# The delta rule's keys turned token-major by VectorE block transposes and a DRAM round trip instead of by TensorE

## The chip, the cores and the metric

One core of a Trainium2 chip runs the whole kernel. The metric is the device time of one execution in microseconds (us); a kernel is judged by the median of several executions. In rows of the profile PE is TensorE's matmul, PEld its weight load, DVE is VectorE, ACT is ScalarE, POOL is GpSimd, and SP is SyncE, which issues nearly all DMAs here.

## The reference, cut to what matters

One layer of a hybrid decoder block, 1024 tokens, model width 1024, everything in float32. The input projection `h @ W_in` gives the columns of two mixers; the first one is a gated delta rule with 8 heads of width 128.

```python
qkv = causal_dwconv_silu(concatenate([qa, ka, va]), conv_w)      # 4 taps along the tokens
k_dn = l2_normalize(ka.reshape(b, s, 8, 128))                    # x * rsqrt(sum(x*x) + EPS)
g    = -exp(a_log) * softplus(a_in + dt_bias);  beta = sigmoid(beta_in)
# chunks of tokens, gc = cumsum(g) in a chunk, decay[i, j] = exp(gc[i] - gc[j]) for j <= i
lmat  = where(strict, (k * beta) @ k.T * decay, 0)
t_inv = inverse(eye + lmat)
u, w  = t_inv @ (v * beta), t_inv @ (k * beta * exp(gc))
a_qk  = q @ k.T * decay
k_dec = k * exp(gc[-1] - gc)
for each chunk:                                                  # state: 128 x 128 per head
    v_new = u - w @ state
    o     = (q * exp(gc)) @ state + a_qk @ v_new
    state = state * exp(gc[-1]) + k_dec.T @ v_new
```

Then `rms_norm(o) * silu(z)` goes through a projection, a dilated window attention (the second mixer) through another, both are gated, added, sent through `w_out`, added to the input and normalized.

## The kernel before, in words

**The work on TensorE.** Every big product is split in two float32r halves and done as three matmuls of 128x128 by 128x512 (`three`, line 557; the tiles `pj`). `projections` (line 724) runs one unit of 48 such matmuls after another in the order of the list `prog`: for each pair of heads p the keys k0 and k1, then q, v, z tiles and some gates; then the attention's tiles; then the products behind both mixers. Weights come by DMA into `wr` (2 tiles) and are split by ScalarE and VectorE into `wh` (6 tiles). A unit's result leaves PSUM by ScalarE and, for q, k and v, by three VectorE multiply-adds (`conv`, line 577).

**The delta rule** of a head is a set of generators ("streams"). The keys leave `conv` channel-major: 128 channels on partitions, 1024 tokens along the free axis. `k_stream` (line 896) needs them token-major, as `kp` (128 tokens of a chunk on partitions, 8 chunks of 128 channels along the free axis), for two things: the sum of squares of each token (`kss`, which gives `s_all` and `ds_all`, the normalized beta and its decayed form) and the weights of the state update. It does this by 8 TensorE transposes into two PSUM tiles `sb`; ScalarE takes 8 squares with a running sum, and copies the two halves to `kp`; GpSimd multiplies `kp` by `ds_all`. `d_stream` makes the decay tile, `n_stream` multiplies keys by keys (and on VectorE by `s_all`), `inv_stream` inverts 32x32 blocks of two heads at once on VectorE (31 steps), `merge_stream` puts them together to the inverse `TT`, `q_stream` and `qsum_stream` do the same for the queries, and `v_stream` turns the values token-major by `turn` (line 1082): a VectorE block transpose, a DMA to DRAM and four DMAs back, which end in another order of the free axis (4 blocks of 32 channels outermost). `rec_stream` (line 1107) then walks over 8 chunks: two products with the state (`kt`, `qt` by `st`), a VectorE step to `r`, a product with `TT`, a ScalarE copy to `w`, two products with `kp` and the attention tile `at`, and a VectorE step to the next state. The two heads of a pair run in each other's gaps.

**What sets the order.** The kernel runs no scheduler on the chip. While it is written, `Sched` (line 103) keeps a clock for each engine, books each instruction with a cost (`book`, line 123), and lets the ready stream of the lowest priority number go on; `projections` has number 99 and fills what is left. Each engine then has its instructions in that order and waits at each only for its own inputs. What a stream does there is bound by tile slots: `Slots.get` (line 60) waits until a tile is free, and with `add=n` until more than `debt + n` are free. The pool `big` has 34 tiles of 128x1024; a key projection asks with `add` 4 or 3 (`out_store`, line 696), since the streams of its pair will take that many, and a head gives five tiles back when its last chunk is written:

```python
        while len(self.free_at) <= (0 if add is None else self.debt + add):   # 62, Slots.get
        add = dict(kA=4 - idx % 2, qA=1, qB=(4, 0, 4, 0, 4, 0)[idx % 6]).get(kind, 0)   # 699
        big.put(5)                                                            # 1163, rec_stream
```

Of the kernel before, what the change touches and what calls it, by code (L numbers as in the profile page):

```python
# [7 lines left out]
F32 = mybir.dt.float32  # L8
F32R = mybir.dt.float32r
AF = mybir.ActivationFunctionType  # L10
OP = mybir.AluOpType
AX = mybir.AxisListType
# [3 lines left out]
P = 128  # L16
T = 1024
D = 1024
H = 8
# [233 lines left out]
def hybrid_block_kernel(ctx: ExitStack, tc: tile.TileContext, x, c, norm_w, ada_w, ada_b, w_tiles, w_vb0, w_vb1,  # L253
# [3 lines left out]
    pe, act, dve, pool, sp = S.pe, S.act, S.dve, S.pool, S.sp  # L257
# [9 lines left out]
    dp = ctx.enter_context(tc.tile_pool(name="dram", bufs=1, space=DRAM))  # L267
    ctx.enter_context(tc.manual_schedule())

    big = Slots(S, bigp, "big", NBIG, [P, T])  # L270
# [5 lines left out]
    sb = Slots(S, sbp, "sb", 4, [P, 512])  # L276

    def const(shape, name, dtype=F32):
        return cp.tile(shape, dtype, name=name)
# [3 lines left out]
    ident, upper, later, ones = cst[:, 0:128], cst[:, 128:256], cst[:, 256:384], cst[:, 384:512]  # L283
# [18 lines left out]
    ds_all = const([P, 64], "ds_all")  # L302
# [11 lines left out]
    fg_d = [dp.tile([32, P], F32, name=f"fgd{g}") for g in range(3)]  # L314
    g_d = dp.tile([64, P], F32, name="grow")
    ot_d = [dp.tile([P, T], F32, name=f"otd{h}") for h in range(H)]
    vt_d = [dp.tile([P, T], F32, name=f"vtd{h}") for h in range(H)]
    st_d = dp.tile([T, 3, 8], F32, name="std")

# [546 lines left out]
    kss = const([P, H, 8], "kss")  # L866
# [4 lines left out]
    junk2 = const([P, P], "junk2")  # L871
# [24 lines left out]
    def k_stream(h):  # L896
        yield ev_k[h]
        yield ev_stats
        kt = KT[h]
        hs = slice(h * 8, h * 8 + 8)  # L900
        kp = yield from big.get(owed=1)
        for hf in range(2):
            pb = yield from sb.get()
            for i in range(4):
                pe.transpose(pb[:, i * P:(i + 1) * P], kt[:, (4 * hf + i) * P:(4 * hf + i + 1) * P], ident)
            yield
            for i in range(4):
                act.activation(junk2, pb[:, i * P:(i + 1) * P], AF.Square, accum_out=kss[:, h, 4 * hf + i:4 * hf + i + 1])
            act.activation(kp[:, hf * 512:hf * 512 + 512], pb, AF.Copy)
            sb.put()  # L910
        yield
        t = ik[:, h]
        dve.tensor_scalar(t, kss[:, h], EPS, None, op0=OP.add)
        dve.reciprocal(s_all[:, hs], t)
        dve.tensor_tensor(s_all[:, hs], s_all[:, hs], beta[:, hs], op=OP.mult)
        dve.tensor_tensor(ds_all[:, hs], s_all[:, hs], dec[:, hs], op=OP.mult)
        S.set(ev_s[h])
        yield
        pool.tensor_tensor(t, t, pw[:, 1], op=OP.pow)
        kp3 = kp.rearrange("p (a b) -> p a b", a=8)  # L920
        pool.tensor_tensor(kp3, kp3, ds_all[:, hs, None].to_broadcast([P, 8, P]), op=OP.mult)
        KP[h] = kp
        S.set(ev_kp[h])

# [157 lines left out]
    def turn(src, dst, bounce):  # L1082

        t = yield from big.get()
        dve.transpose(t.rearrange("p (j i d) -> p i j d", j=4, i=8), src.rearrange("p (i j d) -> p i j d", i=8, j=4))
        yield
        sp.dma_start(bounce, t)
        big.put()  # L1090
        yield
        bv = bounce.rearrange("(b r) (j f) -> j r b f", b=4, j=4)
        for j in range(4):
            sp.dma_start(dst[32 * j:32 * j + 32, :].rearrange("r (b f) -> r b f", b=4), bv[j])
        yield
# [540 lines left out]
    for h in range(H):  # L1636
        S.add(rec_stream(h), 3 + h * 0.01, f"rec{h}")
        S.add(merge_stream(h), 3.5 + h * 0.01, f"merge{h}")
        S.add(v_stream(h), 4 + h * 0.01, f"v{h}")
        S.add(q_stream(h), 4.2 + h * 0.01, f"q{h}")  # L1640
        S.add(qsum_stream(h), 4.3 + h * 0.01, f"s{h}")
        S.add(n_stream(h), 4.4 + h * 0.01, f"n{h}")
        S.add(k_stream(h), 4.6 + h * 0.01, f"k{h}")
        S.add(d_stream(h), 4.8 + h * 0.01, f"d{h}")
# [78 lines left out]
```

## Time and profile before

| What | Value |
|---|---|
| median of three executions | 1302.91 us (1300.87 to 1303.49) |
| the profiled execution | 1300.81 us, of which its span is 1299.0 us |
| TensorE matmul busy | 1261.6 us (97% of the span) |
| VectorE, ScalarE, GpSimd busy | 690.9, 494.3 and 145.4 us |
| DMA | 137.65 MB, 106 GB/s in the mean |
| granted TensorE clock, mean | 0.994 |

All engine instructions are recorded through one helper, so that every row names line 96; rows are told apart by their tiles. `pj<-big,wh` is a matmul of a projection, `sb<-cst,big` a transpose (of h at the start, of the keys later), `sb<-big` keys by keys, `sb<-sq,big` and `sb<-sq,TT` the recurrence of a head, `sb<-qpart,cst` the sum of the queries' squares, `vtd` and `otd` the DRAM tiles through which values and outputs are turned, `grow` a row of decays that is spread over partitions. A float32 matmul of 128x128 stands as two records. The time of the profiled execution is 2.1 us under the median.

### The profile page before, as it was taken

What the parts mean: (1) busy time and instruction counts of PE and PEld (TensorE: products, weight loads), DVE (VectorE), ACT (ScalarE), POOL (GpSimd) and SP (SyncE); (2) the same over time, 40 slices, a digit from 0 to 9 for tenths busy, and PEclk for the clock granted to TensorE, in tenths of its full rate; (3) what the DMA queues carried; (4) which work ended last, traced back from release to release, by engine and by line L of the source; (5) the groups of instructions that cost most, each with busy time, mean ns of one, the idle gap of its engine ahead of it and who ended that gap; (6) DMA issues with size and microseconds to landing.
All of it is one profiled execution on the core that took longest, in us unless ns stands there. A gap on an engine that the chain in (4) does not pass through costs nothing.

```text
span 1299.0 us, 18858 instructions
## 1 busy us (share of the span) xinstructions
PE 1261.6 (97%) x7386; PEld 1049.0 (81%) x7386; DVE 690.9 (53%) x1437; ACT 494.3 (38%) x1054; POOL 145.4 (11%) x97
## 2 busy tenths in 40 slices
PE   5799899999999999999999999999999999999997
PEld 3698678988888988888888888777777888888886
DVE  6766682377763468843778533232322147645433
ACT  5637312455234362234542242453536342222211
POOL 4601200023000221001310002000000000002400
PEclk9899999999999999999999999999999999999999
DMA  9335532163321433231522226211100257333422
GB/s 362 120 123 179 95 93 58 33 197 94 95 70 40 149 125 93 78 102 33 179 74 73 82 66 194 66 35 65 35 33 33 83 187 208 102 127 117 156 95 89
DMA packets 76138, 137.65 MB, mean 106 GB/s; under 512 B 30193, under 2 KB 43921, under 8 KB 76050
## 3 DMA queue, kind: packets, MB, share of 16 engines
q1 hardware_dynamic: 75906, 136.20, 33.2%
q8 instruction: 58, 0.95, 0.3%
q14 instruction: 30, 0.25, 0.1%
q10 hardware_dynamic: 144, 0.26, 0.1%
HBM read 105.84 MB, written 30.59 MB: 105 GB/s over the span
## 4 chain that ended last, share of the span: by engine, by line
PE 82%; issue 7%; DVE 6%; DMA 3%; POOL 1%; ACT 1%; SPq 0%; POOLq 0%; DVEq 0%; ACTq 0%
PE pj L96 69%; PE sb L96 13%; DVE big L96 4%; DMA big<-in_x_dram 1%; DMA vtd<-big 1%; DVE wh L96 1%; POOL big L96 1%; DVE mod L96 1%; DMA big<-grow 0%; ACT big L96 0%; DVE mid L96 0%; DMA big<-otd 0%; SPq L96 0%; POOL mo L96 0%; DMA otd<-big 0%
## 5 line engine op out<-in xcount | busy, mean ns | idle before, releaser
L96 PE MATMUL pj<-big,wh 128*128 128x512 f32 x3840 | 941.8, 398 | 11.2 <-POOL big L96 6.4
L96 PEld LDWEIGHTS pj<-big,wh 128*128 128x128 f32 x3840 | 706.3, 189 | 157.5 <-POOL big L96 7.8
L96 ACT ACTIVATE wh<-wr 128x1024 fp32r<-128x1024 f32 (+3 forms) x96 | 95.6, 996 | 316.1 <-PE pj L96 292.4
L96 DVE TENSOR_TENSOR wh<-wr,wh 128x1024 fp32r<-128x1024 f32 (+3 forms) x93 | 115.5, 1243 | 148.1 <-ACT wh L96 147.9
L96 ACT ACTIVATE big<-big 128x1024 f32<-128x1024 f32 (+1 forms) x61 | 64.5, 1059 | 147.2 <-DVE big L96 115.7
L96 PE MATMUL pj<-wh,big 128*128 128x256 f32 (+2 forms) x702 | 109.5, 307 | 0.0
L96 PEld LDWEIGHTS pj<-wh,big 128*128 128x128 f32 x702 | 95.9, 189 | 5.2 <-DVE big L96 0.2
L96 DVE SCALAR_TENSOR_TENSOR big<-pj,cw,big 128x1023 f32<-128x1023 f32 (+2 forms) x66 | 84.4, 1279 | 1.8 <-ACT big L96 0.3
L96 PEld LDWEIGHTS sb<-sq,big 128*128 128x128 f32 x464 | 62.6, 191 | 4.4
L96 PE MATMUL sb<-sq,big 128*128 128x128 f32 x464 | 65.5, 274 | 0.0
L96 DVE TENSOR_TENSOR big<-big,big 128x1024 f32<-128x1024 f32 (+3 forms) x40 | 55.2, 1388 | 15.1 <-ACT big L96 13.0
L96 ACT ACTIVATE big<-pj 128x1024 f32<-128x1024 f32 (+1 forms) x56 | 51.7, 923 | 21.3 <-PE pj L96 21.2
L96 ACT ACTIVATE mid<-sb 128x384 f32<-128x384 f32 (+5 forms) x75 | 34.1, 461 | 66.8 <-PE sb L96 66.4
L96 POOL TENSOR_TENSOR wh<-wr,wh 128x1024 fp32r<-128x1024 f32 x3 | 8.4, 2785 | 399.0 <-ACT wh L96 399.0
L96 ACT ACTIVATE mid<-mid,sta 128x128 f32<-128x128 f32 (+1 forms) x96 | 42.2, 441 | 25.5 <-DVE sta L96 25.4
L96 DVE COPY big<-sb 128x256 f32<-128x256 f32 (+1 forms) x32 | 12.4, 389 | 74.0 <-PE sb L96 73.9
L96 DVE SCALAR_TENSOR_TENSOR sq<-sq,gsm,sb 128x128 f32<-128x128 f32 x48 | 16.5, 345 | 63.2 <-PE sb L96 61.8
L96 PE MATMUL pj<-big,big 128*128 128x512 f32 x210 | 49.1, 389 | 0.0
L96 ACT ACT_TABLE_LOAD x29 | 37.2, 1283 | 28.8 <-DVE big L96 23.9
L96 PE MATMUL sb<-big,big 128*128 128x128 f32 (+4 forms) x365 | 45.5, 316 | 2.0 <-DVE big L96 2.0
L96 PEld LDWEIGHTS pj<-big,big 128*128 128x128 f32 x210 | 39.4, 188 | 8.2
L96 DVE TENSOR_TENSOR mid<-big 64x31 f32<-64x31 f32 (+15 forms) x124 | 41.1, 332 | 9.0 <-POOL big L96 5.6
(124 smaller groups left out, 1086.3 us busy)
## 6 DMA issues: line engine op xcount, KB each, us to landing
wr<-in_w_tiles_dram SPq DMA_DIRECT2D x64, 512.0 KB, 3.9
big<-in_ada_w_dram SPq DMA_DIRECT2D x24, 512.0 KB, 9.0
big<-in_x_dram SPq DMA_DIRECT2D x16, 512.0 KB, 5.0
gd<-big SPq DMA_DIRECT2D x16, 512.0 KB, 5.0
big<-gd SPq DMA_DIRECT2D x16, 512.0 KB, 4.7
big<-grow SPq DMA_DIRECT2D x8, 512.0 KB, 5.6
vtd<-big SPq DMA_DIRECT2D x8, 512.0 KB, 3.0
big<-vtd SPq DMA_DIRECT2D x32, 128.0 KB, 3.8
```

The lines of the kernel that those rows point to most:

```text
L96: r = f(*a, **k)
```

## The change

`k_stream` turns its keys by `turn`, through a new DRAM tile `kt_d[h]` per head, into a tile `kr`. The sums of squares come from one ScalarE square of the whole tile (into `kp`, as scratch) and one VectorE reduction over both inner axes; GpSimd's multiply reads `kr` in the new order and writes `kp` in the old one. The 8 transposes, 8 squares with running sum and 2 copies of each head go.

```diff
+    kt_d = [dp.tile([P, T], F32, name=f"ktd{h}") for h in range(H)]
...
         yield ev_stats
         kt = KT[h]
         hs = slice(h * 8, h * 8 + 8)
+        kr = yield from big.get()
+        yield from turn(kt, kr, kt_d[h])
         kp = yield from big.get(owed=1)
-        for hf in range(2):
-            pb = yield from sb.get()
-            for i in range(4):
-                pe.transpose(pb[:, i * P:(i + 1) * P], kt[:, (4 * hf + i) * P:(4 * hf + i + 1) * P], ident)
-            yield
-            for i in range(4):
-                act.activation(junk2, pb[:, i * P:(i + 1) * P], AF.Square, accum_out=kss[:, h, 4 * hf + i:4 * hf + i + 1])
-            act.activation(kp[:, hf * 512:hf * 512 + 512], pb, AF.Copy)
-            sb.put()
+        act.activation(kp, kr, AF.Square)
+        yield
+        dve.tensor_reduce(kss[:, h], kp.rearrange("p (b a d) -> p a b d", b=4, a=8), AX.XY, OP.add)
...
         pool.tensor_tensor(t, t, pw[:, 1], op=OP.pow)
-        kp3 = kp.rearrange("p (a b) -> p a b", a=8)
-        pool.tensor_tensor(kp3, kp3, ds_all[:, hs, None].to_broadcast([P, 8, P]), op=OP.mult)
+        pool.tensor_tensor(kp.rearrange("p (a b d) -> p b a d", a=8, b=4), kr.rearrange("p (b a d) -> p b a d", b=4, a=8),
+                           ds_all[:, None, hs, None].to_broadcast([P, 4, 8, 32]), op=OP.mult)
+        big.put()
```

A head so issues one DMA of 512 KB to DRAM and four of 128 KB back, all on SP. Since `Sched` books other instructions, the order on all engines moves from the first pair's keys on.

VectorE, first pair of heads, around the queries' sums of squares, before. `mid` is the queries' squares and `qpart` their sums, `big<-pj,cw,big` the multiply-adds of a projected tile, `big<-sb,s_all,big` the products keys by keys or queries by keys.

```order
L96 TENSOR_TENSOR wh_1315<-wr_1084,wh_1314 128x1024
L96 SCALAR_TENSOR_TENSOR big_1285<-sb_1303,s_all,big_1122 128x128 x4
L96 SCALAR_TENSOR_TENSOR big_1191<-pj_1192,cw,big_1191 128x1023
L96 SCALAR_TENSOR_TENSOR big_1191<-pj_1192,cw,big_1191 128x1022
L96 SCALAR_TENSOR_TENSOR big_1191<-pj_1192,cw,big_1191 128x1021
L96 STREAM_TRANSPOSE mid_1353<-mid_1324 128x512
L96 TENSOR_REDUCE qpart<-mid_1353 128x16
L96 SCALAR_TENSOR_TENSOR big_1120<-sb_1348,s_all,big_1120 128x128 x4
L96 STREAM_TRANSPOSE big_1394<-big_1191 128x8x4x32
L96 SCALAR_TENSOR_TENSOR big_1122<-sb_1389,s_all,big_1122 128x128 x4
L96 SCALAR_TENSOR_TENSOR big_1120<-sb_1366,s_all,big_1120 128x128 x4
L96 STREAM_TRANSPOSE mid_1413<-mid_1396 128x512
```
Now; the `mod` rows are the last of the adaptive scale's dot products, `kss` is the new reduction:

```order
L96 SCALAR_TENSOR_TENSOR big_1168,mod<-big_1119,big_246 128x1024
L96 TENSOR_TENSOR mod<-mod,adab 128x1
L96 TENSOR_SCALAR mod<-mod 128x8
L96 STREAM_TRANSPOSE mid_1230<-mid_1224 128x512
L96 TENSOR_REDUCE qpart<-mid_1230 128x16
L96 STREAM_TRANSPOSE mid_1253<-mid_1241 128x512
L96 TENSOR_REDUCE qpart<-mid_1253 128x16
L96 TENSOR_TENSOR wh_1246<-wr_1092,wh_1245 128x1024
L96 SCALAR_TENSOR_TENSOR big_1173<-pj_1174,cw,big_1173 128x1023
L96 SCALAR_TENSOR_TENSOR big_1173<-pj_1174,cw,big_1173 128x1022
L96 SCALAR_TENSOR_TENSOR big_1173<-pj_1174,cw,big_1173 128x1021
L96 TENSOR_REDUCE kss<-big_1258 128x8
```
The queries' sums stood behind two of the products with `s_all`; now they stand ahead of the keys' sums and of all these products.

SP, the same place, before (`rowd` is a row that waits for VectorE's `mod`, `ktd` the keys' new DRAM tile, `nd` the input of the inversion):

```order
L96 DMA big_1120<-grow 128x1024
L96 DMA big_1122<-grow 128x1024
L96 DMA big_1129<-in_ada_w_dram 128x1024
L96 DMA rowd<-mod 128x8x1
L96 DMA vtd_158<-big_1225 128x1024
L96 DMA wr_1251<-in_w_tiles_dram 128x1024
L96 DMA big_960<-vtd_158 32x4x256 x4
L96 DMA nd_110<-big_1268 32x8x32 x4
```
Now:

```order
L96 DMA big_1102<-grow 128x1024
L96 DMA big_1104<-grow 128x1024
L96 DMA big_1119<-in_ada_w_dram 128x1024
L96 DMA ktd_158<-big_1097 128x1024
L96 DMA ktd_159<-big_1100 128x1024
L96 DMA rowd<-mod 128x8x1
L96 DMA wr_1179<-in_w_tiles_dram 128x1024
L96 DMA big_1096<-ktd_158 32x4x256 x4
L96 DMA big_1099<-ktd_159 32x4x256 x4
L96 DMA wr_1282<-in_w_tiles_dram 128x1024
L96 DMA nd_110<-big_1325 32x8x32 x4
```
The keys are written to DRAM at once, and their way back stands behind `rowd` and a weight load.

TensorE, heads 6 and 7, in the sixth of eight chunks, before. `TT_101` and `TT_100` are the inverses of the two heads; rows with `sq` as first input are the recurrence.

```order
L96 MATMUL sb_6746<-sq_6736,TT_101 128x128
L96 MATMUL pj_6711<-big_364,wh_6307 128x512 x2
L96 MATMUL sb_6750<-sq_6741,TT_100 128x128
L96 MATMUL pj_6711<-big_365,wh_6307 128x512 x2
L96 MATMUL sb_6758<-sq_6752,big_5725 128x128
L96 MATMUL sb_6758<-sq_6752,big_5543 128x128
L96 MATMUL sb_6761<-sq_6756,big_5621 128x128
L96 MATMUL sb_6761<-sq_6756,big_5454 128x128
L96 MATMUL pj_6711<-big_364,wh_6308 128x512 x2
L96 MATMUL pj_6711<-big_403,wh_6307 128x512 x2
L96 MATMUL sb_6775<-sq_6764,big_5538 128x128
L96 MATMUL sb_6775<-sq_6764,big_6044 128x128
```
Now:

```order
L96 MATMUL sb_6752<-sq_6746,TT_101 128x128
L96 MATMUL sb_6754<-sq_6749,TT_100 128x128
L96 MATMUL sb_6760<-sq_6756,big_5732 128x128
L96 MATMUL sb_6760<-sq_6756,big_5490 128x128
L96 MATMUL sb_6763<-sq_6758,big_5645 128x128
L96 MATMUL sb_6763<-sq_6758,big_5405 128x128
L96 MATMUL sb_6773<-sq_6766,big_5485 128x128
L96 MATMUL sb_6773<-sq_6766,big_5948 128x128
L96 MATMUL sb_6777<-sq_6769,big_5403 128x128
L96 MATMUL sb_6777<-sq_6769,big_5577 128x128
L96 MATMUL sb_6786<-sq_6780,TT_101 128x128
L96 MATMUL sb_6788<-sq_6783,TT_100 128x128
```
Before, projection matmuls (`pj`, two in a row) stand between all steps of the recurrence, in every chunk of every pair. Now the last chunks of each pair follow each other with no projection between them: 19 rows of the recurrence in the first pair, 10 in the second, 37 in the third and 51 in the fourth, 10 rows to a chunk of both heads. At these places the projections' stream was waiting for slots of `big`, which the recurrence gives back at its end.

## The prediction

> **What bounds the kernel now.** I read the page first: busy shares, then the chain that ended last.
>
> ```profile
> span 1299.0 us, 18858 instructions
> PE 1261.6 (97%) x7386; PEld 1049.0 (81%) x7386; DVE 690.9 (53%) x1437; ACT 494.3 (38%) x1054; POOL 145.4 (11%) x97
> PE 82%; issue 7%; DVE 6%; DMA 3%; POOL 1%; ACT 1%; SPq 0%; POOLq 0%; DVEq 0%; ACTq 0%
> ```
>
> TensorE is busy for 97% of the span and carries 82% of the chain. So only two things count: how long TensorE's own work takes, and where it stands idle. Its idle places near the change come from the waits (us in total, times, longest), the windows (us; then busy time with count of PE, PEld, DVE, ACT and POOL; granted clock, DMA share, GB/s) and the timeline (start, duration, engine, work).
>
> ```profile
> PE sb L96 <- DVE qpart L96: 4.7, 1, 4.7
> PE sb L96 <- DVE big L96: 2.0, 2, 1.5
> ...
> 150.00:200.00 50.00, 43.65 (x197) 35.48 (x198) 40.73 (x100) 9.33 (x11) 1.41 (x2) 0.97 0.30 90
> 158.00:164.00 6.00, 1.26 (x14) 0.71 (x12) 5.93 (x18) 2.49 (x4) 0.15 (x1) 1.00 0.35 131
> 164.00:168.00 4.00, 4.00 (x18) 3.22 (x19) 3.79 (x13) 0.18 (x1) 0.00 (x0) 0.57 0.49 135
> ...
> 149.85 1.12 DVE L96 SCALAR_TENSOR_TENSOR big<-sb,s_all,big 128x128 f32<-128x128 f32 x4
> 151.11 1.13 PE L96 MATMUL sb<-big,big 128*128 128x128 f32 x8 [1.49 <-DVE big L96]
> 163.92 0.25 PE L96 MATMUL sb<-qpart,cst 128*32 128x8 f32 x8 [4.74 <-DVE qpart L96]
> ```
>
> In the first pair TensorE waits 2.0 us for VectorE to drain products and 4.7 us for the queries' sums. After the 4.7 us idle the granted clock is 0.57 for 4 us, against 1.00 in the 6 us ahead of it. The chain shows what made VectorE late there: the values' turn, `132.17 11.31 DMA vtd<-big`, quoted below.
>
> Last, one chunk of the recurrence, heads 6 and 7, well covered by projections:
>
> ```profile
> 757.00:777.00 20.00, 20.00 (x127) 17.89 (x126) 7.83 (x25) 9.54 (x33) 0.00 (x0) 1.00 0.16 54
> ...
> 759.08 1.06 PE L96 MATMUL sb<-sq,big 128*128 128x128 f32 x8
> 759.80 0.73 DVE L96 SCALAR_TENSOR_TENSOR sq<-sb,gsm,big 128x128 f32<-128x128 f32 x2 [0.89 <-PE sb L96]
> 760.18 0.74 ACT L96 ACTIVATE big<-sb,gsm 128x128 f32<-128x128 f32 x2 [0.78 <-DVE sq L96]
> 760.89 0.38 PE L96 MATMUL sb<-sq,TT 128*128 128x128 f32 x2
> 761.31 0.28 ACT L96 ACTIVATE sq<-sb 128x128 f32<-128x128 f32 x1 [0.38 <-PE sb L96]
> 762.27 1.05 PE L96 MATMUL sb<-sq,big 128*128 128x128 f32 x8
> 762.91 0.35 DVE L96 SCALAR_TENSOR_TENSOR sq<-sq,gsm,sb 128x128 f32<-128x128 f32 x1 [2.38 <-PE sb L96]
> 764.09 1.06 PE L96 MATMUL sb<-sq,big 128*128 128x128 f32 x8
> ```
>
> TensorE is full (20.00 of 20) although each step waits for VectorE or ScalarE: projections fill the gaps. A chunk of both heads takes 764.09 − 759.08 = 5.0 us.
>
> **1. The transposes leave TensorE.**
>
> ```profile
> 110.40 7.08 PE L96 MATMUL pj<-big,wh 128*128 128x512 f32 x30
> 117.32 1.91 PE L96 MATMUL sb<-cst,big 128*128 128x128 f32 x16
> 118.98 16.59 PE L96 MATMUL pj<-big,wh 128*128 128x512 f32 x72
> ```
>
> Sixteen transposes, two heads', stand between 117.32 and 118.98, 1.66 us, or 0.104 us each. All 64: 64 × 0.104 = **−6.6**. The last record's tail overlaps the next projection, so 1.91/16 × 64 = 7.6 is the upper bound of the gain.
>
> By the Trainium skill, page "TensorE: Matmul & The Clock Gate", section "Part 4: PE-mode transpose", a 128x128 transpose (measured there in bf16) takes some 275 ns inside a kernel; by that figure the term would be 64 × 0.275 = 17.6 us. The row decides against it: sixteen float32 ones in a stream take 1.66.
>
> **2. The first pair.** In the new order the queries' sums stand ahead of the keys' sums and of the value turn's wait on VectorE. Its rows:
>
> ```profile
> 113.62 1.23 DVE L96 TENSOR_TENSOR wh<-wr,wh 128x1024 fp32r<-128x1024 f32 x1 [1.25 <-ACT wh L96]
> 114.87 3.91 DVE L96 SCALAR_TENSOR_TENSOR big<-pj,cw,big 128x1023 f32<-128x1023 f32 x3
> 118.69 1.21 DVE L96 SCALAR_TENSOR_TENSOR big<-big,big 128x1024 f32<-128x1024 f32 x1
> 121.22 2.63 DVE L96 TENSOR_TENSOR_SCAN big<-big,cst 128x128 f32<-128x128 f32 x8 [1.11 <-DMA big<-grow]
> 130.90 1.24 DVE L96 STREAM_TRANSPOSE big<-big 128x1024 f32<-128x1024 f32 x1
> 156.88 0.70 DVE L96 STREAM_TRANSPOSE mid<-mid 128x512 f32<-128x512 f32 x1
> 157.61 0.69 DVE L96 TENSOR_REDUCE qpart<-mid 128x16 f32<-128x512 f32 x1
> ```
>
> From 114.87 VectorE now has: one tile's multiply-adds 3.9, two turns 2.5, a dot product 1.2, two scans 5.3, a weight split 1.2, multiply-adds 3.9, a dot product 1.2, both queries' squares 2 × 1.4; with some 0.6 of small ones it ends at about 137.5. TensorE gets there after the 117.3 of its row above and 88 records of projection at 16.59/72 = 0.23, about 137. So a wait of 0 to 2 is left; I take 0.9. What goes: 2.0 + 4.7 of waits, and the low clock, 4 us at 0.57, which is 4 × 0.43 = 1.7. Together −8.4 + 0.9 = **−7.5**; if the old waits come back elsewhere, 0.
>
> **3. Waits of the key transposes.** Later pairs' transposes wait for ScalarE's silu of the keys, which now only VectorE's turn needs:
>
> ```profile
> PE sb L96 <- ACT big L96: 1.3, 2, 0.8
> ```
>
> **−1.3**.
>
> **4. Chunks without cover.** This is the price. The new order has 19, 10, 37 and 51 rows of the recurrence with no projection among them, 10 rows to a chunk: 11.7 chunks. The keys' way is longer, the planner's projections have meanwhile taken more of `big`, and run into `Slots.get` until the recurrence gives tiles back at its end. A bare chunk lasts as long as its own chain. From the rows at 759: products with the state until VectorE can start, 759.80 − 759.08 = 0.72; that step 0.36 (half of 0.73); hand-over to TensorE 0.14 (149.85 + 1.12 = 150.97 to 151.11); product with `TT` until ScalarE starts 0.42 (760.89 to 761.31); its copy 0.28, or 0.48 if half of the two output copies of 0.74 still stands ahead; hand-over 0.14; 762.27 to 762.91, 0.64; VectorE 0.35; hand-over 0.14. Sum 3.2 to 3.4. TensorE's own work in it:
>
> ```profile
> L96 PE MATMUL sb<-sq,big 128*128 128x128 f32 x464 | 65.5, 274 | 0.0
> ```
>
> Eight records at 759.08 end after 1.06, the last being 0.27 long: (1.06 − 0.27)/7 = 0.11 each, 20 to a chunk, 2.2. So a bare chunk leaves TensorE idle for 1.0 to 1.2 us: 12 to 14 over 11.7 chunks. The steps at the edges, with one or two pairs of projection rows to fill gaps, cost 2 to 3 more: **+17**. Bounds: 0.97 × 11.7 = 11 with the heads well interleaved, and 33 if a chunk keeps its covered 5.0 us (2.8 × 11.7).
>
> The same page, section "A second HAM failure mode: psum-queue depth-cycling", says that short idles between groups of matmuls, when frequent enough, make TensorE's clock swing between half and full. The rows here show the clock falling after one idle of 4.74 us, not after the 1.49 us ahead of it. That rule is the third rival below.
>
> **5. The normalized beta comes later.** It gates the drain of keys by keys. The old path: eight squares and a copy per half on ScalarE. The new one: turn, write, read, square, reduction.
>
> ```profile
> L96 ACT ACTIVATE junk<-sb x64: 257/278/283, 118.0 to 654.5; 128x128 f32<-128x128 f32 x64
> L96 ACT ACTIVATION_READ_ACCUMULATOR junk<-sb x64: 192/194/219, 118.1 to 654.7; 128x1 f32 x64
> 119.42 0.59 ACT L96 ACTIVATE big<-sb 128x512 f32<-128x512 f32 x1
> ...
> vtd<-big SPq DMA_DIRECT2D x8, 512.0 KB, 3.0
> big<-vtd SPq DMA_DIRECT2D x32, 128.0 KB, 3.8
> ...
> 132.17 11.31 DMA vtd<-big
> ...
> rowd<-mod SPq DMA_DIRECT2D x1, 4.0 KB, 12.2
> ```
>
> Old, per head: 8 × (0.28 + 0.19) + 2 × 0.59 = 4.9. New: 1.24 + 3.0 + 3.8 + a square of the tile, about 1.06 as an estimate from ScalarE's other rows of this size (the page's group `big<-big` of 128x1024), + a reduction, 0.69 × 2 = 1.4 from the queries' half-size row: 10.5 us. In the first pair the way back also stands on SP behind `rowd`, whose 4 KB took 12.2; the 11.3 of the values' write just behind it ended about when `rowd` did (130.3 + 12.2 = 142.5 against 143.5). `rowd` now is issued at about 134, so these keys land at 138 by the short time, or at 147 behind it; then the first drained tile comes at 154, where TensorE, with the four PSUM tiles of `sb` all taken by keys by keys, arrives at about 153. Waits of 0 to 2 there; in the later pairs 6 us more on a path which the projections cover until the merge. I take **+2**; bounds 0 and 16, the latter 4 per pair if the inverse were late everywhere.
>
> **What I cost at nothing.** ScalarE loses 8 × 4.9 = 39 us and gains 8.5 (38% busy). VectorE gains 8 × (1.24 + 1.4) = 21 us at 53% busy; it lies under TensorE's projections, and without that cover is worth 2 × 2.6 = 5 per pair. 8.4 MB of extra DMA run at a mean share of a third. GpSimd's multiply, now strided (the row was `125.84 2.00 POOL`), makes `kp`, which the recurrence reads over 50 us later; were it three times as long, it still ended ahead:
>
> ```profile
> 125.84 2.00 POOL L96 TENSOR_TENSOR big<-big,ds_all 128x1024 f32<-128x1024 f32 x1
> ```
>
> **The sum.** The profiled execution took 1300.8 (span 1299.0). 1300.8 − 6.6 − 7.5 − 1.3 + 17 + 2 = 1304.4. The median shown, 1302.9, is 2.1 above the profiled one, so the forecast for the median is 1304.4 + 2.1 = **1306**: 0.3% slower.
>
> **Rivals.**
> - *The gains win.* The bare chunks cost their low bound 11 and nothing at the edges, the wait at the queries' sums is 0 and term 5 is 0: −6.6 − 8.4 − 1.3 + 11 = −5, median 1298. For it: the two heads interleave well in the rows at 759, and the output copies are not in the chain. Against: each bare chunk has five hand-overs to wait for, which no work covers. It decides from 1.0 us of idle per bare chunk downwards.
> - *The turn is late everywhere.* If the write takes the 11.3 us of the first values' turn rather than 3.0, the keys' products stall TensorE on `sb` with about 4 per pair: +14 in place of +2, 1318 to 1320. For it: the row at 132.17. Against: the median of eight such writes is 3.0, and only that one stood behind `rowd`.
> - *The clock falls in the bare chunks.* Half clock doubles 2.2 us of work in each, of which 1.1 exceeds the idle: 1.1 × 11.7 = 13, and some 1.7 to recover in each of four pairs: 1306 + 13 + 7 = 1326. For it: 0.57 at 164. Against: only an idle of 4.7 us brought it, and bare chunks idle 1.2 at most in all.
> - *The bare stretches do not arise* because the projections are ahead on the chip as well: the order is fixed when the kernel is written, so I give this no chance of its own.
>
> **How the numbers follow.** Forecast 0.50 (its own range 1301 to 1313, by the bounds of terms 2, 4 and 5 varied one at a time); the gains win 0.27; the late turn 0.16; the clock 0.07. The range from 1295 to 1320 leaves out most of the clock case, the far end of the second and the best of the first: some 0.2. A measurement of this kernel tells about 0.2%, 2.6 us, from no change, so "same" is 1300.3 to 1305.5. Faster: nearly all of the first rival and a little of the forecast, 0.29. Same: somewhat under half of the forecast, 0.22. Slower: the rest of the forecast, 0.26, and the last two cases, 0.23: 0.49.
>
> **What would show it.** In the changed profile: 64 rows `sb<-cst,big` rather than 128, ScalarE about 30 us less busy and VectorE about 20 more; no wait of 4.7 at `qpart` and a clock of 1.00 over the first pair; new waits of TensorE on VectorE's and ScalarE's `sq`, in stretches of some 6, 3, 12 and 17 us at the ends of the four pairs' recurrences, 1.0 to 1.2 per chunk and 14 to 17 in all. The forecast is wrong if those waits are under 10 in all (then it is faster), if TensorE waits on `big` or `TT` for more than 5 (the late turn), or if the granted clock in those stretches is under 0.9.

## The result and the profile after

| What | Before | Changed |
|---|---|---|
| median | 1302.67 us (a fourth execution added to the three above) | 1313.6 us (1309.92 to 1314.02, four executions) |
| ratio | | 1.0086, 95% interval 1.0074 to 1.0098 |
| the profiled execution | 1300.81 us | 1309.92 us, span 1308.1 us |
| mean granted clock of it | 0.994 | 0.996 |
| TensorE transposes among `sb<-cst,big` | 128 | 64 |

The changed kernel is 0.9% slower. The forecast was 1306, in a range of 1295 to 1320. The page of the changed kernel, its first rows and its chain:

```profile
span 1308.1 us, 18695 instructions
PE 1262.8 (97%) x7322; PEld 1045.7 (80%) x7322; DVE 710.5 (54%) x1453; ACT 471.5 (36%) x918; POOL 147.3 (11%) x97
PE 78%; DMA 8%; DVE 7%; ACT 3%; issue 2%; POOL 1%; SPq 1%; POOLq 0%; DVEq 0%; ACTq 0%
```

VectorE has 19.6 us more, ScalarE 22.8 us less, and the span follows neither. TensorE's share of the chain fell from 82 to 78%, and DMA's rose from 3 to 8%: the keys' round trip is now on the chain. TensorE's waits in the changed kernel (us in total, times, longest):

```profile
PE sb L96 <- ACT sq L96: 6.3, 5, 1.9
...
PE sb L96 <- ACT qss L96: 2.6, 1, 2.6
...
PE sb L96 <- DVE sq L96: 2.1, 6, 0.8
PE sb L96 <- DVE qpart L96: 1.7, 2, 1.0
```

The 4.7 at `qpart` is down to 1.0, as forecast. The waits on `sq` are the chunks without cover; the one on `qss` was not forecast.

Where the time went can be read by looking, in both traces, at the start of the same projection matmul, at places where TensorE has done the same other work in both (transposes of keys aside). The times are of the two profiled executions.

| Projection matmuls gone by | Before, us | Changed, us | Step, us | What lies in it | Forecast |
|---|---|---|---|---|---|
| 64 | 57.7 | 56.5 | −1.2 | the start, which the change doesn't touch (see below) | 0 |
| 404 | 119.0 | 116.3 | −1.5 | first pair's key transposes | −1.7 |
| 556 | 170.3 | 164.0 | −3.7 | first pair's products and queries' sums | −7.5 |
| 974 | 270.4 | 268.3 | +4.3 | first pair's merge and recurrence | +2.8 |
| 1166 | 322.7 | 318.3 | −2.3 | second pair's keys and products | −1.4 |
| 1684 | 447.9 | 446.7 | +3.2 | second recurrence | +1.5 |
| 1902 | 505.0 | 504.4 | +0.6 | third pair's keys and products | −1.4 |
| 2274 | 618.0 | 623.4 | +6.0 | third recurrence | +5.4 |
| 2652 | 714.0 | 716.8 | −2.6 | fourth pair's keys and products | −1.4 |
| 2844 | 784.8 | 793.3 | +5.8 | fourth recurrence | +7.4 |
| 4490 | 1221.3 | 1230.3 | +0.5 | the rest | 0 |

The forecast column splits the prediction's terms by their places: the bare chunks by their rows, 17 / 117 each; term 1 evenly over the four pairs, terms 3 and 5 over the three later ones. The first step is luck of the two executions: ahead of this place the clock was at half twice for 3.4 us in the kernel before and once in the changed one, a difference of some 1.4 us up to here. Recurrences: +19.2 (forecast +17). Keys and products of pairs two to four: −4.3 (forecast −4.2). First pair up to its products: −5.2 (forecast −9.2). The steps end at +9.0, the spans differ by 9.1.

The fourth pair's uncovered end, TensorE alone (start, duration, work, idle before it):

```profile
774.20 0.75 PE L96 MATMUL sb<-sq,TT 128*128 128x128 f32 x4 [0.76 <-DVE sq L96]
775.07 2.32 PE L96 MATMUL sb<-sq,big 128*128 128x128 f32 x16
777.45 0.87 PE L96 MATMUL sb<-sq,TT 128*128 128x128 f32 x4
778.39 2.32 PE L96 MATMUL sb<-sq,big 128*128 128x128 f32 x16
...
785.05 2.32 PE L96 MATMUL sb<-sq,big 128*128 128x128 f32 x16
...
789.54 0.71 PE L96 MATMUL sb<-sq,big 128*128 128x128 f32 x4 [0.22 <-DVE sq L96]
```

From 775.07 to 785.05 there are three chunks of both heads, 3.33 us each: the chain that the prediction put at 3.2 to 3.4. In the first pair, on three engines:

```profile
134.84 12.62 SPq L96 DMA_DIRECT2D big<-ktd  x8
137.50 0.25 PE L96 MATMUL sb<-qpart,cst 128*32 128x8 f32 x8 [1.04 <-DVE qpart L96]
149.84 1.06 ACT L96 ACTIVATE big<-big 128x1024 f32<-128x1024 f32 x1 [12.81 <-DMA big<-ktd]
150.80 0.16 ACT L96 ACTIVATE qss<-sb 128x8 f32<-128x8 f32 x1
151.01 1.42 PE L96 MATMUL sb<-big 128*128 128x128 f32 x8 [2.64 <-ACT qss L96]
...
148.00:152.00 4.00, 1.36 (x11) 1.17 (x10) 1.07 (x1) 1.12 (x2) 0.00 (x0) 0.97 1.09 239
152.00:156.00 4.00, 4.00 (x14) 3.20 (x13) 2.32 (x9) 3.43 (x4) 0.73 (x1) 0.60 0.06 23
```

The keys come back at 149.8. ScalarE has waited 12.81 us for them in front of the square, and behind the square stands the copy of the queries' sums, which TensorE finished at 137.7. That copy frees a PSUM tile of `sb`, and TensorE waits 2.64 us for it. Behind this wait the clock is granted at 0.60 (the windows' columns are those of the prediction). These two, 2.64 and 4 × 0.40 = 1.6, are what the first pair gained less (3.8 us).

### The profile page after: what moved, and what is told of

Read it like the earlier page. It is cut to its first block, busy times and chain, and to the rows that moved or that the text cites. A ratio compares the mean times of both kernels' runs of the same rounds, so it can differ in the third digit from the quotient of the medians.

```text
span 1308.1 us, 18695 instructions
## 1 busy us (share of the span) xinstructions
PE 1262.8 (97%) x7322; PEld 1045.7 (80%) x7322; DVE 710.5 (54%) x1453; ACT 471.5 (36%) x918; POOL 147.3 (11%) x97
## 4 chain that ended last, share of the span: by engine, by line
PE 78%; DMA 8%; DVE 7%; ACT 3%; issue 2%; POOL 1%; SPq 1%; POOLq 0%; DVEq 0%; ACTq 0%
PE pj L96 65%; PE sb L96 13%; DVE big L96 4%; DMA big<-ktd 3%; DMA big<-otd 2%; ACT big L96 2%; SPq L96 1%; DVE wh L96 1%; POOL big L96 1%; DMA ktd<-big 1%; DMA wr<-in_w_out_dram 1%; DMA big<-in_x_dram 1%; DMA otd<-big 1%; DVE mod L96 1%; POOL wh L96 1%
## 5 line engine op out<-in xcount | busy, mean ns | idle before, releaser
L96 PE MATMUL pj<-big,wh 128*128 128x512 f32 x3840 | 922.0, 395 | 12.1 <-POOL big L96 5.8
L96 DVE TENSOR_TENSOR wh<-wr,wh 128x1024 fp32r<-128x1024 f32 (+3 forms) x93 | 107.5, 1157 | 132.2 <-ACT wh L96 132.1
L96 ACT ACTIVATE big<-big 128x1024 f32<-128x1024 f32 (+1 forms) x69 | 72.8, 1059 | 177.0 <-DVE big L96 126.4
L96 PE MATMUL pj<-wh,big 128*128 128x256 f32 (+2 forms) x702 | 113.0, 309 | 0.3 <-POOL wh L96 0.3
L96 PE MATMUL sb<-sq,big 128*128 128x128 f32 x464 | 68.2, 281 | 7.7 <-ACT sq L96 6.3
L96 DVE TENSOR_TENSOR big<-big,mid 64x31 f32<-64x31 f32 (+15 forms) x124 | 41.6, 335 | 4.2
```

The source lines that it names most:

```text
L96: r = f(*a, **k)
```

## Experiments

Each ratio is to the kernel before, run on the same chip in the same job (medians 1301.1, 1300.6 and 1301.05 in the three jobs). All kernels compute the whole reference.

**Cover for the recurrences.** Only the order of projections changes: gate tiles (`g`) move to the ends of the first three pairs' lists, ahead of the next pair's keys (one of them from the second pair to the third), and one of the attention's z tiles (`Z`, six of which came later) goes behind the fourth pair. The few lines that read `Z` are left out.

```diff
-    "q0 B0 v0 q1 v1 z0 g g z1 g g B1",
-    "k0 k1 q0 v0 z0 g v1 q1 z1 g g B2",
-    "k0 k1 q0 v0 z0 g q1 v1 g g z1 g",
-    "k0 k1 q0 v0 z0 g q1 v1 z1 g g g",
+    "q0 B0 v0 q1 v1 z0 g g z1 B1 g g",
+    "k0 k1 q0 v0 z0 g v1 q1 z1 g B2 g",
+    "k0 k1 q0 v0 z0 g q1 v1 z1 g g g g",
+    "k0 k1 q0 v0 z0 g q1 v1 z1 g g g Z",
```

> The changed kernel with another order of projections: gates, and one of the attention's z tiles, are moved ahead of the next pair's keys, so that TensorE has projections while a recurrence ends; the keys' new way is untouched, and no chunk of a recurrence is left without projection rows. Theory (uncovered chunks cost 19 us): 1313.6 - 19 = about 1295, at most 4 more for projections that the attention then lacks. Rival (the recurrence is late because the turn is late, whatever stands around it): TensorE waits as long at other instructions, 1310 to 1316.

> The kernel before with the same order of projections as in the run covered. It has no uncovered chunk before or after. Theory: nothing to gain there, 1301 to 1306. If the new order were better by itself, and not by what it covers: as much faster here as in covered.

Measured: covered 1300.44, ratio 1.0001 (0.9987 to 1.0015); the old key way in that order 1299.89, ratio 0.9992 (0.9984 to 1.0001). So the order by itself is worth at most 0.2%, and in the changed kernel it gives 0.85%, some 11 us. The waits on `sq` come to 0.7 us in all. The theory's 1295 was missed by 5. The waits and windows of the profiled execution show what was lost in it, which is one of the four longest of the twelve (1305.35, mean clock 0.987; the median ones have 0.991):

```profile
PE sb L96 <- DMA Xb<-xd: 4.1, 2, 3.8
...
PE sb L96 <- ACT qss L96: 2.9, 1, 2.9
...
204.00:208.00 4.00, 1.03 (x23) 0.92 (x24) 1.23 (x3) 0.00 (x0) 0.00 (x0) 0.95 0.29 51
208.00:212.00 4.00, 4.00 (x29) 3.94 (x27) 2.26 (x6) 0.75 (x2) 0.00 (x0) 0.50 0.19 30
224.00:228.00 4.00, 4.00 (x27) 3.88 (x27) 1.10 (x2) 0.62 (x2) 0.00 (x0) 0.50 0.00 0
```

The first pair's inverse (`Xb<-xd`) comes 3.8 us too late for its merge, and the clock is at half for 20 us behind it, worth 10. How much of that the other executions lost was not recorded; by their mean clock it was less.

**The 4 KB DMA ahead of the keys.** In the first pair the keys' way back stands on SyncE behind `rowd`. First it was postponed in the code, in both kernels, and the planner ordered anew:

```diff
-        sp.dma_start(row_d.rearrange("o (j p) -> p (o j)", p=P), mod[:, 16:24])
         big.put()
+        yield ev_T[1]
+        sp.dma_start(row_d.rearrange("o (j p) -> p (o j)", p=P), mod[:, 16:24])
```

> The changed kernel, with the 4 KB DMA to rowd issued only after the first inverse is done, so that the first pair's keys do not stand behind it. Theory (they wait for it: the reads took 14 us): their landing moves from about 149 to 139 to 142, ScalarE's square no longer holds up the copy of the queries' sums, TensorE's wait of 2.6 at 151 and the low clock at 151.8 go: -4.4, so 1309. Rival (the reads are slow by themselves or by the weight load ahead of them): landing stays near 149, time within 1 us of 1313.6.

> The kernel before with the same postponed DMA. Theory: the first values' write takes 3 to 4 us instead of 11.3, VectorE's idle of 9.16 at 148.7 goes, and with it the waits 2.0 and 4.7 of TensorE and the low clock at 164: -6 to -8, so 1295 to 1297. Rival (the write is slow for another reason): within 1 us of 1302.7.

In the kernel before the theory held: 1293.44, ratio 0.9948 (0.9933 to 0.9963). VectorE's wait for the values is 0.84 us instead of 9.16, and TensorE's on `qpart` is gone. The row in the kernel before, then in this run:

```profile
148.70 1.23 DVE L96 TENSOR_TENSOR big<-big,ik 128x1024 f32<-128x1024 f32 x1 [9.16 <-DMA big<-vtd]
...
140.90 1.22 DVE L96 TENSOR_TENSOR big<-big,ik 128x1024 f32<-128x1024 f32 x1 [0.84 <-DMA big<-vtd]
```

In the changed kernel it brought nothing: 1311.44, ratio 1.0087 (1.0068 to 1.0105). The keys did come back early, but the planner, which was told of the later DMA as well, now placed the keys' squares between those of the queries, and TensorE waited 3.8 us for the queries' sums in place of the 2.6 for their copy. Rows of that run, its wait and its DMA to landing (min/median/max; 14.0 at most in the changed kernel):

```profile
PE sb L96 <- DVE qpart L96: 4.0, 2, 3.8
...
DMA to landing us min/median/max: 2.6/4.7/6.0
```

So the DMA was postponed without telling the planner, which leaves every engine's order as it was, except for that one row on SyncE:

```diff
-        sp.dma_start(row_d.rearrange("o (j p) -> p (o j)", p=P), mod[:, 16:24])
+        S.book("dma", "dma_start", row_d.rearrange("o (j p) -> p (o j)", p=P), (), {})
...
             sp.dma_start(xb[32 * b:32 * b + 32, :, off:off + 32], xv[i, b])
+        if h == 1:
+            nc.sync.dma_start(row_d.rearrange("o (j p) -> p (o j)", p=P), mod[:, 16:24])
```

> The changed kernel with every engine's order as it is, except that SyncE issues the 4 KB DMA to rowd after the first inverse is read back (the planner is told that it stands where it stood). Theory (that DMA alone holds the first pair's keys back): the reads land at about 140 instead of 149, TensorE's wait of 2.6 on the queries' sums' copy at 151 and the low clock at 151.8 go, 4.4 us: ratio to the kernel before 1.005. Rival (the price is in the longer path as such): landing early, time as the changed kernel, ratio 1.0086.

> The run covered with the same postponed DMA and nothing else. There the first pair's merge waited 3.8 us for the inverse at 206.6 and the clock was low for 20 us behind it, some 13 us in all, and 2.9 were lost at the queries' sums' copy. Theory (the inverse was late only because the keys were): both go, ratio 1.000 - 0.011 = 0.989 (about 1287). Rival (the merge now comes too early for the longer key path, whatever is done at rowd): the wait stays above 2 us, ratio above 0.996.

Measured in the changed kernel: 1311.61, ratio 1.0078 (1.0066 to 1.0090). By the trace the mechanism is right: the copy of the queries' sums starts at 138.57 instead of 150.80, the wait on `qss` is gone, and the projection matmul that started at 154.8 starts at 151.2, after a start that was 0.7 us later: −4.3. The step of the first pair's products in the table is −8.3 here, in place of −3.7. But behind the first merge the clock is at half for 10.2 us, worth 5.1, which gives the gain back:

```profile
138.57 0.16 ACT L96 ACTIVATE qss<-sb 128x8 f32<-128x8 f32 x1
...
212.00:216.00 4.00, 3.29 (x78) 2.82 (x77) 0.00 (x0) 2.49 (x4) 0.00 (x0) 0.93 0.40 161
216.00:220.00 4.00, 3.94 (x20) 3.83 (x20) 1.79 (x3) 0.39 (x2) 0.00 (x0) 0.50 0.67 225
```

With cover as well: 1292.8, ratio 0.9940 (0.9926 to 0.9954), between the two expectations. The wait for the inverse fell from 4.1 to 1.3 us, so the inverse was late because the keys were. The profiled execution is the longest of the six (1296.89, mean clock 0.990; the others took 1289.8 to 1294.9 at 0.993 to 0.996). Most of what it lacks to 1287 is a low clock of 13.7 us, worth 6.8, behind a stall of 1.47 us for which the trace shows no cause ("issue"):

```profile
207.57 0.44 PE L96 MATMUL sb<-Xb,big 64*64 64x64 f32 x4 [1.47 <-issue]
...
212.00:216.00 4.00, 4.00 (x23) 3.66 (x23) 1.09 (x2) 0.00 (x0) 0.00 (x0) 0.50 0.00 0
```

**The price of uncovered chunks alone.** The kernel before, with two gates held back until a recurrence is done:

```diff
+        after = {("gB", 2): 4, ("gB", 6): 6}.get((kind, idx))
+        if after is not None:
+            yield [ev_ttfree[after], ev_ttfree[after + 1]]
         st[i] = yield from big.get(add=add)
```

> The kernel before, in which two projection units (one gate each in the third and in the fourth pair) are held back until that pair's recurrence is done: 62 rows of recurrence (6.2 chunks) then have no projections among them; keys are turned by TensorE as before. Theory: such chunks cost what they cost in the changed kernel, 19.2 / 11.7 = 1.64 each: +10, ratio 1.008. Rival (they were dear only in company with the DRAM turn's work on VectorE and the queues): 0 to +4, ratio up to 1.003.

Measured: 1312.87, ratio 1.0095 (1.0082 to 1.0108). The steps, at the same places as in the table, are +5.9 in the third and +5.3 in the fourth recurrence, +0.3 between them and nothing elsewhere: 11.5 for 62 rows, 1.9 per chunk, somewhat above the theory's 1.64. The rows are those of the changed kernel, in a kernel that has no DRAM turn of keys:

```profile
596.05 0.61 PE L96 MATMUL sb<-sq,TT 128*128 128x128 f32 x4
598.17 2.32 PE L96 MATMUL sb<-sq,big 128*128 128x128 f32 x16 [1.51 <-ACT sq L96]
600.54 0.87 PE L96 MATMUL sb<-sq,TT 128*128 128x128 f32 x4
601.50 2.32 PE L96 MATMUL sb<-sq,big 128*128 128x128 f32 x16
604.22 0.75 PE L96 MATMUL sb<-sq,TT 128*128 128x128 f32 x4 [0.41 <-DVE sq L96]
```

A chunk lasts 601.50 − 598.17 = 3.33 again, and 1.5 are lost on entering.

**Is the planner to blame, or the path?** The keys' DMAs are issued, but not booked:

```diff
-    def turn(src, dst, bounce):
+    def turn(src, dst, bounce, q=sp):
...
-        yield from turn(kt, kr, kt_d[h])
+        yield from turn(kt, kr, kt_d[h], nc.sync)
```

(and `q.dma_start` in `turn`).

> The changed kernel, but the planner is not told of the keys' DMAs (they cost it nothing), so that it orders the work almost as if the keys were turned at once; 37 rows of recurrence stay without projections (third pair). Theory (the loss comes from the order that the planner makes of a longer path; the path itself has slack): bare chunks cost 6 instead of 19, so 1313.6 - 13 = about 1300, ratio 0.998, if waits of TensorE at the keys' products stay under 3 us. Rival (the path has no slack, so that an order which ignores it meets the wait in another place): waits of TensorE on VectorE's or DMA's results grow by 8 to 15, ratio 1.004 to 1.010.

Measured: 1322.58, ratio 1.0163 (1.0150 to 1.0176); the waits came in another place, as the rival said, and cost more than it said. The waits of this run, then three rows of its fourth pair:

```profile
PE sb L96 <- ACT big L96: 11.8, 2, 11.4
...
PE sb L96 <- DVE qpart L96: 6.8, 1, 6.8
...
PE pj L96 <- DVE big L96: 4.1, 2, 3.7
...
660.98 1.06 ACT L96 ACTIVATE big<-big 128x1024 f32<-128x1024 f32 x1 [13.50 <-DMA big<-ktd]
672.78 1.06 ACT L96 ACTIVATE big<-big 128x1024 f32<-128x1024 f32 x1 [8.37 <-DMA big<-ktd]
681.25 2.07 PE L96 MATMUL sb<-big,big 128*128 128x128 f32 x8 [11.43 <-ACT big L96]
```

An order that counts on quick keys meets them late at the products; the planner's bare chunks are the cheaper form of the delay. How much slack the path itself has is not shown by this run: in its order ScalarE's silu of the second head's keys (663.35) stands behind the first head's square, which waits for its DMA, so that the second turn starts at 664.44, the two round trips follow each other and the squares stand 11.8 us apart. Other work for TensorE hides the delay, as the run covered showed.

**One part alone.** The DRAM turn for the first pair only (`if h < 2`, else the old code), and for the other three only (`if h >= 2`).

> Only the first pair's keys (heads 0 and 1) go by the DRAM turn, those of the other six heads by TensorE as before. 19 rows of recurrence without projections, in the first pair. Theory (the parts add up, each pair pays for itself): by the steps seen between the two kernels in the first pair, -1.5 for the transposes, -3.7 for the waits that go, +4.3 for the bare chunks: -0.9, ratio 0.999. Rival (the loss builds up from pair to pair): the first pair alone costs nothing or gains its whole 5, ratio under 0.997.

> The other part: the keys of heads 2 to 7 go by the DRAM turn, the first pair's by TensorE. 103 rows of recurrence without projections (15, 37 and 51). Theory: bare chunks of those pairs, 10.3 at 1.52 each (14.9 us for 98 rows in the changed kernel) = +15.7, transposes and the waits at them -6.5, later products +1.5: +10.7, ratio 1.008; together with p0 that is the changed kernel's 1.0086. Rival (one pair's delay moves the others): ratio under 1.005 or over 1.011.

Measured: 1302.58, ratio 1.0007 (0.9998 to 1.0016), and 1314.62, ratio 1.0107 (1.0094 to 1.0120). The first pair pays for itself, the others lose, more than the theory's 1.008 and just inside the rival's 1.011; the excesses add up to 0.0114 against 0.0086 (0.0074 to 0.0098) for all. Some 0.05% of the gap goes with 5 rows more without cover in the second part; the rest is not settled.

**With and without the change under the same good conditions, and the best of both.** The old way with the covering order and the unbooked postponement, and a kernel that turns by DRAM where the first pair's haste isn't in the way:

> The kernel before with the order of projections of the run covered and the postponed DMA of row_same: the old key way under the conditions of the run covered_row_same. Theory (without bare chunks the new way saves its transposes and the waits at them, 8 us, and loses little): 1294 to 1296 here, so slower than covered_row_same (1292.8) by 2 to 5. Rival (the new way has nothing to give even when covered): equal or faster than covered_row_same, 1288 to 1292.

> The first pair's keys by TensorE, the other six heads' by the DRAM turn, gates and one z tile moved so that no chunk of a recurrence is without projections, and the DMA to rowd postponed as in row_same. Theory: the postponed DMA alone gave ratio 0.9948; the transposes of six heads and the waits at them go as well (-6.5), later products cost 1 to 2: ratio 0.991, about 1289, faster than either kernel. Rival (the later pairs too lack slack, so that waits at products or merges eat the gain): ratio 0.994 or more.

The old way: 1299.85, ratio 0.9988 (0.9980 to 0.9997); slower than expected, since the clock is at half for 13.7 us behind its first merge, as in covered_row_same. So the new key way, covered and not held up, is the faster one, by 0.9988 − 0.9940 = 0.48% or 6 us in the medians. A part of that is the clock, whose mean is 0.991 in the median execution of the old way and 0.993 to 0.994 in that of the new one; in the two profiled executions, both with 13.7 us of low clock, the spans are 1297.6 and 1295.0, and 2.6 us are left. The last kernel took the first pair's keys by TensorE, the others by DRAM, with this order and `rowd` postponed as in row_same:

```diff
+        if h < 2:  # the old transposes, squares and copies
...
-    "k0 k1 q0 v0 z0 g v1 q1 z1 g g B2",
-    "k0 k1 q0 v0 z0 g q1 v1 g g z1 g",
-    "k0 k1 q0 v0 z0 g q1 v1 z1 g g g",
+    "k0 k1 q0 v0 z0 g v1 q1 z1 g B2 g",
+    "k0 k1 q0 v0 z0 g q1 v1 z1 g g g g",
+    "k0 k1 q0 v0 z0 g q1 v1 z1 g g g Z",
```

Measured: 1289.17, ratio 0.9911 (0.9898 to 0.9923), as expected, and faster than both kernels (before 1301.05 on that chip). Against the run old_row_late, which has the same old first pair and the same mean clock of 0.996 in its median execution, it is 0.9948 − 0.9911 = 0.37% or 5 us faster. That is the DRAM turn of six heads, covered, together with the other order of projections, which gave the old way at most 0.2%. By the places of the table, from 974 to 4490, behind the first pair, this kernel gains 4.2 us on the kernel before, and old_row_late 0.2. So most of the 0.9% is the postponed DMA. Its page:

```profile
span 1287.5 us, 18728 instructions
PE 1254.3 (97%) x7338; PEld 1044.7 (81%) x7338; DVE 709.5 (55%) x1449; ACT 474.6 (37%) x952; POOL 145.0 (11%) x97
```

## Why the prediction was right, and where it was short

The likeliest case came true: the change saves what was said and pays more in chunks without cover. The sum for the profiled execution was 1304.4; it took 1309.9. Point by point:

1. **Transposes, and the waits at them (−6.6 − 1.3).** Right together with term 5: −1.5 in the first pair and −4.3 in the others, where +2 of later products is contained, against −1.7 and −4.2. The 275 ns of the Trainium skill, page "TensorE: Matmul & The Clock Gate", section "Part 4: PE-mode transpose", would have made it a gain of 17.6; no step shows that.
2. **The first pair (−7.5): mis-sized, −3.7.** The wait at the queries' sums was 1.04, in the bound of 0 to 2. What was left out is that ScalarE, too, works in order: the prediction followed the keys on SyncE to 147 (149.8 it was) and looked for the damage at VectorE's products, not at the copy that stands on ScalarE behind the keys' square and holds an `sb` tile. Run row_same took the cause away: the 2.64 and the low clock behind it went, and the step became −8.3.
3. **Uncovered chunks (+17): right in place and mechanism, +19.2.** The chain of 3.2 to 3.4 was 3.33. The work taken from a covered chunk, put at 2.2, comes out at 2.25 as well. The chunk from 759.08 to 764.09 in the kernel before takes 5.01 and holds twelve records of projection, 16.59/72 = 0.23 each, or 2.76 together:

```profile
759.89 1.16 PE L96 MATMUL pj<-big,wh 128*128 128x512 f32 x4
...
761.03 0.71 PE L96 MATMUL pj<-big,wh 128*128 128x512 f32 x2
...
761.72 0.71 PE L96 MATMUL pj<-big,wh 128*128 128x512 f32 x2
...
763.07 1.18 PE L96 MATMUL pj<-big,wh 128*128 128x512 f32 x4
```

So a bare chunk within a stretch costs 3.33 − 2.25 = 1.08, and 11.7 of them 12.6, as forecast. What was too small is the price of the edges: 19.2 − 12.6 = 6.6 instead of 2 to 3. Entering a stretch costs a wait of 1.8 to 1.9 on ScalarE's copy in three of the four stretches, 5.5 in all, which is why the short stretches cost more than their share and the long one, with 0.76 at its entry, less. Run old_bare shows that this price needs nothing else of the change. One sign was chosen badly: the listed waits on `sq` come to 6.3 + 2.1 = 8.4, under the 10 below which the prediction would have called the kernel faster. The list misses most of the idle inside bare chunks, since each record lasts longer than TensorE needs before the next one may follow (0.28 against 0.11), so that from 770 to 792 it counts as busy for 20.36 of 22 us, at full clock:

```profile
770.00:792.00 22.00, 20.36 (x129) 16.61 (x128) 10.88 (x37) 13.65 (x50) 0.92 (x1) 1.00 0.15 49
```

4. **At nothing:** VectorE +19.6 (21 forecast) and ScalarE −22.8 (about −30) changed no wait of TensorE that the runs could tie to them. The old squares were counted too long: a square and the reading of its sum overlap, and in the kernel before the next square starts 0.40 us later (118.35, 118.75), not 0.28 + 0.19, so a head takes 3.9 and not 4.9; eight heads make up the 8 us. GpSimd's multiply went from 2.01 to 2.05 us and showed up in no new wait of TensorE.
5. **The median** lies 3.7 above the profiled execution instead of 2.1. The other three executions had a mean clock of 0.991 to 0.993, against 0.996; where they lost it was not recorded.

Of the rivals, the gains did not win: the idle per bare chunk was 1.08, and 1.64 with the edges, above the 1.0 from which that would decide. The late turn stayed away from the later pairs (write 3.1 us and read 4.8 in the median), and came in the first pair by way of `rowd`. The clock rival came in a small form: within the bare chunks the clock stayed at 1.00 (the row above), but entering a stretch could lower it. In run row_late (the windows around 605.28, where TensorE had waited 1.94):

```profile
604.00:608.00 4.00, 2.72 (x13) 2.72 (x14) 2.32 (x5) 1.82 (x7) 0.00 (x0) 0.67 0.40 56
608.00:612.00 4.00, 3.71 (x24) 3.15 (x24) 1.76 (x7) 2.15 (x9) 0.00 (x0) 0.90 0.86 337
```

Such a drop lasted 3.4 us here, worth 1.7, where the prediction's rival had the whole stretch at half clock. The profiled execution of the changed kernel has none, although it has the same wait of 1.94 at the same place: the length of the wait alone does not decide it.

## What to carry to other kernels

When a change frees the busiest engine by lengthening a path that feeds it, work out how far the whole order moves back and what work is left to fill the end: here 6.6 us of transposes were paid with 19 us of uncovered chunks. With filler moved there the change cost nothing, and with the small DMA out of the way of the first keys as well it was a gain of some 2 to 6 us over the old way. In an in-order queue, look at what stands behind each new wait, on the engines that seem idle as well: a 0.16 us copy cost 2.6 us and a low clock. A tiny DMA of many small pieces can hold back the large ones behind it on its queue; putting it off was worth 0.5% in the kernel before and 0.6% in the covered one. In the changed kernel, and in the old way with the covering order, it brought under 0.1%: there a low clock or another wait stood in the profile in place of what it took away.

## What the runs showed of the hardware

- A 4 KB DMA of single elements (128 partitions by 8 columns, turned into a row) held up its queue. Behind it, a 512 KB write took 11.3 us (kernel before) and four reads of 128 KB up to 14.0 (changed kernel); without it the longest of the same writes took 5.1 and of the same reads 5.8 to 6.0 (old_row_late, row_same and row_late). In row_same nothing else was moved. Instructions that are fetched meanwhile were slow too: of 390 fetches of 8 KB behind the first 60 us in all fourteen traces, the median took 0.41 us, and the five longest, 2.6 to 3.5, all started within 8 us of this DMA's issue.
- The granted clock fell to half not only after TensorE's idle of 4.7 us, but after shorter ones: 2.64 us at 151 (3.4 us low), and 1.47 us at 207.57 among 32x32 and 64x64 matmuls, after which 13.7 us were low (covered_row_same). The length of the idle does not decide alone: 1.94 us at the entry of the third stretch lowered it in row_late, p123 and unbooked, and not in the changed kernel. Away from the kernel's end the low stretches lasted 3.4, 6.8 (old_row_late), 10.2 (row_same), 13.7 or 20.5 us (covered): multiples of 3.41. Idles of 1.1 us in every 3.33 of bare chunks did not lower it (1.00 from 770 to 792).
- Stalls of TensorE of 0.8 to 1.7 us in or just behind the first merge, which no wait explains, came in five of the six kernels in which `rowd` is postponed, 6 to 15 us behind its issue. The sixth, row_late, issues it at 222.1, when the first merge is over, and has none, and none of the eight kernels that issue `rowd` earlier has one. So they go with this DMA standing at the merge. In old_order27_row a fetch of 16 KB of instructions took 3.6 us there (median 0.99), up to the middle of the stalls; whether late instructions are the cause in all five is open. The last kernel has such a stall (1.1) and no low clock.
